# Hybrid decoder trunk on one core: the last down projection as seven block products with stored weight sums

## The chip, the cores and the metric

The kernel runs on one core of a Trainium2 chip (NeuronCore). A core has a matrix engine (TensorE, PE in the profile), whose weight loads are listed apart as PEld, a vector engine (VectorE, DVE), a scalar engine (ScalarE, ACT), a general engine (GpSimd, POOL) and a queue engine (SyncE, SP). Each engine executes its instructions in the order in which they stand in its queue; a wait of one instruction holds everything behind it. Transfers to and from DRAM are issued by SP, ACT or POOL and run on 16 DMA engines. The metric is the device time of the whole kernel in microseconds (us).

## What is computed

Two decoder layers (`DEPTH = 2`) on 512 rows of 1024 channels, each with a token mixer of three branches and a gated feed-forward, then one RMS norm. The change touches the feed-forward of both layers and the last norm:

```python
def conv_ffn(h, w_up, conv_w, conv_b, w_down):      # D_FF = 2816
    u = h @ w_up                                      # (512, 1024) @ (1024, 5632)
    c = conv_b + causal depthwise convolution of width 3 over the rows of u
    gate, val = jnp.split(c, 2, axis=-1)
    return (jax.nn.silu(gate) * val) @ w_down         # (512, 2816) @ (2816, 1024)

for l in range(DEPTH):
    ...                                               # token mixer, x = x + ... @ w_out
    x = x + conv_ffn(rmsnorm(x, norm2_g[l]), ffn_w_up[l], ...)
return rmsnorm(x, final_g)
```

## The kernel before

Every product in single precision is made of three matmuls on split operands: an operand is a pair of tiles, `hi` (rounded to the matmul format) and `lo` (the remainder), and `mm3` issues lo times hi, hi times hi and hi times lo, each with a 128x128 stationary operand and 512 moving columns.

Weights come through a plan. `unit` hands out the next weight block of 128x512. `load` fetches it with a DMA on SP into one of three raw buffers (`NRAW = 3`, tile `wr`), and `part` splits it: ScalarE casts the raw tile to `hi` (L135), VectorE subtracts (L136) and so frees the raw tile. The results go to pairs of tiles, `wh`/`wl` (three pairs) or `sh`/`sl` (from the pools `f`, `r` or `u`). `AHEAD` says how many units may be split ahead of the one in use. The position of an instruction in its engine's queue is chosen by a scheduler at build time, except where `keep_in_program_order` pins it (in the last stage TensorE is pinned).

The feed-forward has two stages. `ffn_up` makes 44 column blocks (22 pairs of gate and value, channels on partitions, the 512 rows along the free axis); each takes two weight units and 24 matmuls. VectorE multiplies by the norm factor (`fu`, L1054, straight from the accumulator in PSUM), ScalarE starts the convolution (L1056), VectorE adds its two other taps (L1057, L1058) and makes the gated product (`fth`, L1063 and L1064); the product is split into `ah` (L1066, L1067). In the second layer eight blocks of the residual are also turned to row order on the way (`xt`, through DRAM on POOL's queue, L226 and L230). `ffn_down` (first layer) takes 22 of these products for each of 8 column blocks, with weights `wdn`.

The second layer's down projection is `last`. It works with rows on partitions: `act` is the stationary operand, 128 of the 512 rows at a time (four row blocks), and the moving operand is a unit of 512 columns of `wdt`. For the first 512 columns all 22 steps of the inner dimension run over four accumulators in the pool `acc`, then the same for the other 512 columns in four accumulators of the pool `sm`. The last six units (`KEPT = 6`) are held, so that the row blocks end one after the other: each adds the residual (`add`, L1106, four pieces of 128 columns), squares and sums (L1109), gets its factor by a square root (L1137) and a reciprocal (L1138), is scaled and written out. Only the last row block's tail is left when the matmuls are over.

```python
pss = [self.acc() for _ in range(NC)]
for k in range(NFF):
    w = self.unit("wdt", 0, k, 0)
    for c in range(NC):
        prod(pss[c], k, c, w)
```

Of the kernel before, what the change touches and what calls it, by code (L numbers as in the profile page):

```python
# [8 lines left out]
F32 = mybir.dt.float32  # L9
# [15 lines left out]
KEPT = 6  # L25
SEQ = "0 H 0 S 0 U S U S 0 S 0 0 S 2 2 Y 0 0 2 1 2 1 2 1 2 1 2 1 2 1 1 1"
NRAW = 3
AHEAD = {None: 2, "p": 4, "r": 3, "f": 3, "u": 5}
# [20 lines left out]
class Emit:  # L49
# [68 lines left out]
    def load(self, u):  # L118
        name, l, i, c0, n, _ = u
        raw = self.wp.tile([128, 512], F32, name=self.nm("wr"), tag="wr", bufs=NRAW)  # L120
        with self.tc.high_priority():
            self.kept(self.nc.sync.dma_start(raw[:, :n], self.a[name][l, i][:, c0:c0 + n]))
        self.raws.append(raw)
        self.nraw += 1

    def part(self, u):
        raw, n, pool = self.raws.pop(0), u[4], u[5]

        self.turn = (self.turn + 1) % 5 if pool == "p" else 4
        if pool is None or self.turn < 3:  # L130
            hi, lo = [self.wp.tile([128, 512], F32R, name=self.nm(t), tag=t, bufs=3) for t in ("wh", "wl")]
        else:
            hi, lo = [{"f": self.f, "r": self.r, "u": self.u, "p": self.u}[pool](dt=F32R, n=t) for t in ("sh", "sl")]
        with self.tc.high_priority() if pool in (None, "p") else nullcontext():
            self.kept(self.nc.scalar.copy(hi[:, :n], raw[:, :n]))  # L135
            self.kept(self.nc.vector.tensor_tensor(lo[:, :n], raw[:, :n], hi[:, :n], op=SUB))  # L136
# [11 lines left out]
    def mm3(self, ps, w, x, start, stop):  # L148
        (wh, wl), (xh, xl) = w, x

        def mm(*x, **y):
            i = self.nc.tensor.matmul(*x, **y)  # L152
# [79 lines left out]

    def norm_new(self):
# [67 lines left out]
    def run(self):  # L301
        nc, tc, a, V = self.nc, self.tc, self.a, self.nc.vector
        self.con = self.cp.tile([128, NCC], F32, name="con")
        self.rst = self.cp.tile([128, 512], F32, name="rst")
# [729 lines left out]
    def ffn_up(self, l, st, x):  # L1034
# [4 lines left out]
        def at():  # L1039
# [4 lines left out]
        first = self.firstF(l, (78, 79, 80), st, (3,))  # L1044
        for i in range(NFF):
            if x and i % 2 == 1 and i < 17:
# [18 lines left out]
            hi, lo = at(), at()  # L1065
            A.copy(hi, th)  # L1066
            V.tensor_tensor(lo, th, hi, op=SUB)  # L1067
            act.append((hi, lo))
        return act

    def ffn_down(self, l, act, x, st):
# [3 lines left out]
        for m in range(8):  # L1075
# [7 lines left out]
            xd.append(d)  # L1083
        return x, xd


    def last(self, act):


        nc, V, A, P, po = self.nc, self.nc.vector, self.nc.scalar, self.nc.gpsimd, self.tc.keep_in_program_order  # L1090
        fg = [self.u(n="fg") for _ in range(2)]
        for h in range(2):
            nc.sync.dma_start(fg[h], self.a["fgr"][:, 512 * h:512 * h + 512].to_broadcast([128, 512]))
# [3 lines left out]
        def prod(ps, k, c, w):  # L1097
            cs = slice(128 * c, 128 * c + 128)
            ah, al = act[k]
            self.mm3(ps, (ah[:, cs], al[:, cs]), w, k == 0, k == NFF - 1)  # L1100

        def add(y, ps, j, c):

            b = slice(j % 4 * 128, j % 4 * 128 + 128)
            q = lambda t: t[:, b].rearrange("p (a d) -> p a d", d=32)
            return V.scalar_tensor_tensor(q(y), q(ps), 0.5, self.xt[j][:, c], op0=MUL, op1=ADD)  # L1106
# [3 lines left out]

        self.pool = None
        pss = [self.acc() for _ in range(NC)]
        for k in range(NFF):
            w = self.unit("wdt", 0, k, 0)
            for c in range(NC):
                prod(pss[c], k, c, w)
        ya = []
        for c in range(NC):
            y = self.u(n="ya")
            for j in range(4):  # L1120
                add(y, pss[c], j, c)
            square(y, ss[:, c:c + 1])
            P.tensor_tensor(y, y, fg[0], op=MUL)
            ya.append(y)
        V.tensor_scalar(bias, ss, 1.0 / D, 1e-6, op0=MUL, op1=ADD)
        pss = [self.sm() for _ in range(NC)]
        for k in range(NFF - KEPT):
            w = self.unit("wdt", 0, k, 512)
            for c in range(NC):
                prod(pss[c], k, c, w)  # L1130
        self.pool = "u"
        ws = [self.unit("wdt", 0, k, 512) for k in range(NFF - KEPT, NFF)]

# [7 lines left out]
        for c in range(NC - 1):  # L1141
            for k, w in enumerate(ws, NFF - KEPT):
                prod(pss[c], k, c, w)
            y, s = self.u(n="yb"), self.small((128, 1), "fs1")
            for j in range(4, 8):
                po(add(y, pss[c], j, c))
            po(square(y, s))
            rs = factor(s, bias[:, c:c + 1])
            po(A.activation(ya[c], ya[c], AF.Copy, scale=rs))
            nc.scalar.dma_start(self.a["out"][c, :, 0:512], ya[c])  # L1150
            po(V.scalar_tensor_tensor(y, y, rs, fg[1], op0=MUL, op1=MUL))
            nc.sync.dma_start(self.a["out"][c, :, 512:1024], y)
        c, y, b = NC - 1, self.u(n="yb"), bias[:, NC - 1:]
        for k, w in enumerate(ws, NFF - KEPT):
            prod(pss[c], k, c, w)
        for j in range(4, 8):
            po(add(y, pss[c], j, c))
        s = [self.small((128, 1), f"fs{i}", 1) for i in (2, 3)]
        for i in range(2):
            po(square(y[:, 256 * i:256 * i + 256], s[i]))  # L1160
        po(V.scalar_tensor_tensor(b, s[0], 1.0 / D, b, op0=MUL, op1=ADD))
        rs = factor(s[1], b)
        for i in range(2):
            h = slice(256 * i, 256 * i + 256)
            po(V.scalar_tensor_tensor(y[:, h], y[:, h], rs, fg[1][:, h], op0=MUL, op1=MUL))
            nc.sync.dma_start(self.a["out"][c, :, 512 + 256 * i:768 + 256 * i], y[:, h])
            po(A.activation(ya[c][:, h], ya[c][:, h], AF.Copy, scale=rs))
            nc.scalar.dma_start(self.a["out"][c, :, 256 * i:256 * i + 256], ya[c][:, h])
# [114 lines left out]
```

## Time and profile before

| what | value |
|---|---|
| three runs | 1714.98, 1713.65, 1714.87 us; median 1714.87 |
| profiled execution, first to last instruction | 1712.1 us |
| granted TensorE clock, mean | 1.000 |
| matmuls | 10280 |
| DMA, whole execution | 219.61 MB, mean 128 GB/s |
| second layer's `ffn_up`, about | 1359 to 1585.7 us |
| `last`, matmuls | 1585.7 to 1705.5 us |

The runs are timed without the profiler; the span of the profile is one other execution, from its first to its last instruction. The span lies 2.8 us under the median of the runs, which also hold what lies around it. A row of a group of instructions gives busy time, the mean of one in ns, the idle time of the engine just before them, and what ended it. A row of the timeline gives start, duration, engine, line and operation, and in brackets the idle time before it with its releaser. Two instructions of one engine may overlap in these rows, since the engines are pipelined: the distance of the starts says what one more instruction costs.

### The profile page before, as it was taken

What the parts mean: (1) busy time and instruction counts of PE and PEld (TensorE: products, weight loads), DVE (VectorE), ACT (ScalarE), POOL (GpSimd) and SP (SyncE); (2) the same over time, 40 slices, a digit from 0 to 9 for tenths busy, and PEclk for the clock granted to TensorE, in tenths of its full rate; (3) what the DMA queues carried; (4) which work ended last, traced back from release to release, by engine and by line L of the source; (5) the groups of instructions that cost most, each with busy time, mean ns of one, the idle gap of its engine ahead of it and who ended that gap; (6) DMA issues with size and microseconds to landing.
All of it is one profiled execution on the core that took longest, in us unless ns stands there. A gap on an engine that the chain in (4) does not pass through costs nothing.

```text
span 1712.1 us, 27377 instructions
## 1 busy us (share of the span) xinstructions
PE 1701.0 (99%) x10280; PEld 1392.4 (81%) x10280; DVE 1155.0 (67%) x1998; ACT 774.9 (45%) x1315; POOL 178.2 (10%) x213
## 2 busy tenths in 40 slices
PE   9999999999999999999999999999999999999998
PEld 7888777788888888888888888777888888888886
DVE  6887745578669777753368887555776787787333
ACT  6563443554255444433355634345533554444223
POOL 2121000003200000000021210100141011100010
PEclk9999999999999999999999999999999999999999
DMA  5236553525542333233432365535254433333333
GB/s 180 87 109 205 174 174 99 178 89 163 163 148 93 98 99 96 69 113 114 123 105 87 107 222 168 159 122 178 77 185 147 137 122 117 113 109 99 99 99 105
DMA packets 132325, 219.61 MB, mean 128 GB/s; under 512 B 16864, under 2 KB 37088, under 8 KB 132192
## 3 DMA queue, kind: packets, MB, share of 16 engines
q1 hardware_dynamic: 116336, 180.94, 34.4%
q0 software_dynamic: 6784, 20.98, 3.8%
q10 hardware_dynamic: 9072, 15.94, 2.6%
q8 instruction: 81, 1.33, 0.3%
q14 instruction: 52, 0.43, 0.1%
HBM read 188.43 MB, written 29.36 MB: 127 GB/s over the span
## 4 chain that ended last, share of the span: by engine, by line
PE 89%; DMA 5%; DVE 3%; ACT 1%; issue 1%; SPq 1%; ACTq 0%; POOL 0%; DVEq 0%; POOLq 0%
PE acc L152 80%; PE sm L152 4%; PE sm L640 2%; DMA wr<-wall 2%; PE sm L893 1%; DVE wl L136 1%; PE sm L547 1%; DMA ws<-sgw 1%; DMA tr<-yt 0%; DMA tr<-bkT 0%; SPq L226 0%; DMA bkS<-tr 0%; PE sm L998 0%; DMA x<-xT 0%; DMA tr<-qkt 0%
## 5 line engine op out<-in xcount | busy, mean ns | idle before, releaser
L152 PE MATMUL acc<-hi,sh 128*128 128x512 f32 x1108 | 431.9, 390 | 0.0
L152 PE MATMUL acc<-lo,sh 128*128 128x512 f32 x1108 | 431.6, 390 | 0.0
L152 PE MATMUL acc<-hi,sl 128*128 128x512 f32 x1108 | 430.6, 390 | 0.0
L135 ACT CAST sh<-wr 128x512 fp32r<-128x512 f32 (+1 forms) x347 | 212.2, 615 | 356.6 <-PE acc L152 264.3
L136 DVE TENSOR_TENSOR sl<-wr,sh 128x512 fp32r<-128x512 f32 (+1 forms) x347 | 236.1, 683 | 139.9 <-ACT sh L135 74.9
L136 DVE TENSOR_TENSOR wl<-wr,wh 128x512 fp32r<-128x512 f32 x233 | 165.2, 710 | 184.9 <-ACT wh L135 182.3
L135 ACT CAST wh<-wr 128x512 fp32r<-128x512 f32 x233 | 144.1, 619 | 281.1 <-PE acc L152 182.3
L152 PEld LDWEIGHTS acc<-hi,sl 128*128 128x128 f32 x1108 | 208.0, 188 | 43.7 <-DVE gth L1013 0.3
L152 PEld LDWEIGHTS acc<-lo,sh 128*128 128x128 f32 x1108 | 208.0, 188 | 43.6 <-issue 0.9
L152 PEld LDWEIGHTS acc<-hi,sh 128*128 128x128 f32 x1108 | 208.0, 188 | 43.6 <-issue 0.3
L152 PE MATMUL acc<-lo,wh 128*128 128x512 f32 x588 | 232.5, 395 | 0.5 <-DVE lo L211 0.3
L152 PE MATMUL acc<-hi,wl 128*128 128x512 f32 x588 | 230.3, 392 | 0.5 <-DVE wl L136 0.5
L152 PE MATMUL acc<-hi,wh 128*128 128x512 f32 x588 | 229.5, 390 | 0.0
L152 PEld LDWEIGHTS acc<-lo,wh 128*128 128x128 f32 x588 | 110.5, 188 | 26.3 <-DVE lo L211 1.6
L152 PEld LDWEIGHTS acc<-hi,wl 128*128 128x128 f32 x588 | 110.5, 188 | 25.9 <-DVE wl L136 2.3
L152 PEld LDWEIGHTS acc<-hi,wh 128*128 128x128 f32 x588 | 110.6, 188 | 22.4 <-issue 0.2
L152 PE MATMUL acc<-ah,sh 128*128 128x512 f32 x352 | 108.4, 389 | 0.0
L1054 DVE TENSOR_TENSOR fu<-acc,rsF 128x512 f32<-128x512 f32 x88 | 60.6, 688 | 56.4 <-PE acc L152 56.3
L1056 ACT ACTIVATE cv<-fu,pc 128x512 f32<-128x512 f32 x88 | 71.6, 816 | 46.7 <-DVE fu L1054 44.4
L1057 DVE SCALAR_TENSOR_TENSOR cv<-fu,pc,cv 128x511 f32<-128x511 f32 x88 | 65.8, 748 | 21.1 <-ACT cv L1056 20.6
L152 PE MATMUL acc<-wl,hi 128*128 128x512 f32 x192 | 78.3, 408 | 0.0
L152 PEld LDWEIGHTS acc<-ah,sh 128*128 128x128 f32 x352 | 66.1, 188 | 13.7
(312 smaller groups left out, 2345.4 us busy)
## 6 DMA issues: line engine op xcount, KB each, us to landing
wr<-wall SPq DMA_DIRECT2D x488, 256.0 KB, 2.7
gd<-gth ACTq DMA_DIRECT2D x48, 256.0 KB, 3.0
gth<-gd POOLq DMA_DIRECT2D x48, 256.0 KB, 3.6
wr<-wdt SPq DMA_DIRECT2D x44, 256.0 KB, 2.6
wr<-wdn SPq DMA_DIRECT2D x40, 256.0 KB, 2.7
tr<-bkT SPq DMA_DIRECT2D x16, 256.0 KB, 2.8
bkS<-tr SPq DMA_DIRECT2D x128, 32.0 KB, 2.5
tr<-vT SPq DMA_DIRECT2D x8, 256.0 KB, 2.6
```

The lines of the kernel that those rows point to most:

```text
L135: self.kept(self.nc.scalar.copy(hi[:, :n], raw[:, :n]))
L136: self.kept(self.nc.vector.tensor_tensor(lo[:, :n], raw[:, :n], hi[:, :n], op=SUB))
L152: i = self.nc.tensor.matmul(*x, **y)
L547: i = T.matmul(pK[hv[1 - h], j, :], bk[hv[h], c, 1, :], x[hv[h], c, :], start=True, stop=True)
L640: po(T.matmul(o, l, r, start=start, stop=True, skip_group_check=True))
L893: po(T.matmul(X[h][:, i, :], lhsT, rhs, start=new[h], stop=stop, skip_group_check=True))
L1054: V.tensor_tensor(u, ps, self.rsF, op=MUL)
L1056: A.activation(t, u, AF.Identity, scale=self.p("cw2", j), bias=self.p("cb", j))
L1057: V.scalar_tensor_tensor(t[:, 1:], u[:, :511], self.p("cw1", j), t[:, 1:], op0=MUL, op1=ADD)
```

## The change

The down projection of the second layer, `Y = A W` with A of 512x2816 and W of 2816x1024, is cut into 2x2 blocks (rows in halves of 256, columns in halves of 512, the inner dimension in pairs of 128-channel steps), and the eight block products of each pair become seven, with sums of blocks on both sides (the Winograd form of Strassen's scheme). There are 11 pairs `q`, and seven products `p` of each; one product of one pair is a weight unit times two row blocks, that is six matmuls.

- Weight sums. For four of the seven products (`p` = 7, 5, 6, 4) the weight is a combination of the four blocks of the pair. `presum` makes these in the first layer's feed-forward: four loads of 128x512 on POOL's queue, four VectorE operations, four stores to DRAM (`tsum`) on POOL's queue, for one pair at a time (pairs 0 to 3 within `ffn_up`, on 16 tiles of pool `f`; pairs 4 to 10 within `ffn_down`, on tiles of pool `u`).
- Sums of the activations. `halves`, in the second layer's `ffn_up`, makes from two products the row-half combinations: four VectorE operations of 256 columns for a pair, two split operands instead of two, and three stores to DRAM on POOL's queue for what is needed later (`ab`: first row half of both; `s4`).
- `last`. A first pass runs p = 7, 5, 6, 4 over all pairs with eight accumulators (four of `acc`, four of `sm`). Meanwhile `spill` brings the stored `ab` back on POOL's queue and splits it. A second pass adds p = 1 to the accumulators of p = 6, a third runs p = 2, a fourth p = 3, each over 11 pairs. The combinations of the accumulators are made on ScalarE (`half`) and VectorE (`addx`, `plus`, plain additions) during these passes. Two row blocks are finished and written out during the p = 2 and p = 3 passes, with POOL's queue, the other two at the end as before, one after the other.
- Raw buffers. Units of the last stage (plan pool `q`) are fetched up to six ahead (`DEEP = 6`), every other one into a tile of pool `u`, and split four ahead, three pairs of five into `wh`/`wl` and two of five into tiles of pool `u`. The last six units still use the three raw buffers.
- The final gain's load (`fg`) moves from SP's to POOL's queue. `halves` takes its two work tiles from the same three `wh` and three `wl` tiles as the weights.

```diff
+PRE = {(0, "f", 2): 0, ..., (0, "d", 6): 10}
-AHEAD = {None: 2, "p": 4, "r": 3, "f": 3, "u": 5}
+AHEAD = {None: 2, "p": 4, "r": 3, "f": 3, "u": 5, "q": 4}
+DEEP = 6
...
-            while self.nraw < min(self.npart + NRAW, len(self.plan)):
+            while self.nraw < len(self.plan) and self.nraw < self.npart + (DEEP if self.plan[self.nraw][5] == "q" else NRAW):
...
-        raw = self.wp.tile([128, 512], F32, name=self.nm("wr"), tag="wr", bufs=NRAW)
+        raw = self.u(n="wr") if u[5] == "q" and self.nraw % 2 else self.wp.tile([128, 512], F32, name=self.nm("wr"), tag="wr", bufs=NRAW)
+        src = self.tsum[i] if name == "tsum" else self.a[name][l, i]
...
+    def presum(self, l, stage, m):
+        if self.pre:
+            q, b = self.pre.pop()
+            V = self.nc.vector
+            V.tensor_tensor(b[3], b[3], b[1], op=SUB)
+            V.tensor_tensor(b[1], b[1], b[0], op=SUB)
+            V.tensor_tensor(b[0], b[0], b[3], op=ADD)
+            V.tensor_tensor(b[2], b[2], b[0], op=SUB)
+            for p, t in zip((7, 5, 6, 4), (b[3], b[1], b[0], b[2])):
+                self.tsum[q, p] = self.dp.tile([128, 512], F32, name=self.nm("ts"))
+                self.nc.gpsimd.dma_start(self.tsum[q, p], t)
+        q = PRE.get((l, stage, m))
+        if q is not None:
+            b = self.fpre.pop(0) if stage == "f" else [self.u(n="pre") for _ in range(4)]
+            for i, t in enumerate(b):
+                self.nc.gpsimd.dma_start(t, self.a["wdt"][0, 2 * q + i // 2][:, i % 2 * 512:i % 2 * 512 + 512])
+            self.pre.append((q, b))
...
+    def halves(self, a, b, q, at):
+        V, P, h = self.nc.vector, self.nc.gpsimd, [slice(0, 256), slice(256, 512)]
+        s, d = [self.wp.tile([128, 512], F32, name=self.nm(t), tag=t, bufs=3) for t in ("wh", "wl")]
+        ab = self.dp.tile([128, 512], F32, name=self.nm("ab"))
+        ...
+        P.dma_start(ab[:, h[0]], a[:, h[0]])
+        P.dma_start(ab[:, h[1]], b[:, h[0]])
+        V.tensor_tensor(s[:, h[0]], a[:, h[1]], b[:, h[1]], op=ADD)
+        V.tensor_tensor(s[:, h[1]], s[:, h[0]], a[:, h[0]], op=SUB)
+        V.tensor_tensor(d[:, h[0]], b[:, h[0]], s[:, h[1]], op=SUB)
+        P.dma_start(self.s4[:, h[q % 2]], d[:, h[0]])
+        V.tensor_tensor(b[:, h[0]], a[:, h[0]], a[:, h[1]], op=SUB)
+        return self.split(s, at), self.split(b, at), ab, self.s4
...
+        def spill(src, n):
+            o = self.u(n="sp")
+            nc.gpsimd.dma_start(o[:, :n], src[:, :n])
+            hi, lo = self.f(dt=F32R, n="hi"), self.f(dt=F32R, n="lo")
+            A.copy(hi[:, :n], o[:, :n])
+            V.tensor_tensor(lo[:, :n], o[:, :n], hi[:, :n], op=SUB)
+            return hi, lo
...
+        for q in range(Q):
+            s, t = act[q][:2]
+            for p in (7, 5, 6, 4) if q < Q - 1 else (6, 7, 5, 4):
+                w = unit(p, q)
+                x, at = {7: (t, 0), 5: (s, 0), 6: (s, 256), 4: (t, 256)}[p]
+                for r in range(2):
+                    prod(pss[p][r], x, at, r, w, q == 0, q == Q - 1)
+            ...
+            if q:
+                ab.append(spill(act[q - 1][2], 512))
...
+        for q in range(Q):
+            ...
+            w = unit(1, q)
+            for r in range(2):
+                go(1, q, r, w)
+            ...
+            if q < 2:
+                v[2, q], v[3, q] = addx(pss[5][q], 1, 2 + q), addx(pss[5][q], 1, q)
+            elif q < 4:
+                v[1, q - 2] = addx(pss[4][q - 2], 0, q)
...
+        self.pool = "u"
+        ws = [unit(3, q) for q in range(Q - KEPT, Q)]
+        for r in range(2):
+            for q, w in enumerate(ws, Q - KEPT):
+                go(3, q, r, w)
+            ...
+            po(plus(y, out[3][r], y))
```

More of the change, by code (lines that the diff above doesn't have):

```diff
@@ L1102, in add, with unit, prod @@
[L1102 to L1106, printed above, removed]
+        def unit(p, q):
+            if p > 3:
+                return self.unit("tsum", 0, (q, p), 0)
+            return self.unit("wdt", 0, 2 * q + (p > 1), 512 * (p == 3))
+        def prod(ps, x, at, r, w, first, end, **kw):
+            cs = slice(at + 128 * r, at + 128 * r + 128)
+            self.mm3(ps, (x[0][:, cs], x[1][:, cs]), w, first, end, **kw)
@@ L1108, in square, with plus @@
+        def plus(y, ps, z):
+            return V.scalar_tensor_tensor(y, ps, 0.5, z, op0=MUL, op1=ADD)
         def square(y, s):
             return A.activation(self.u(n="sq")[:, 0:y.shape[1]], y, AF.Square, accum_out=s)
[L1111 to L1124, printed above, removed]
@@ L1139, in factor @@
             return rs
[L1141 to L1168, printed above, removed]
+        pss = {p: [(self.acc if p in (7, 5) else self.sm)() for _ in range(2)] for p in (7, 5, 6, 4)}
@@ new lines, in last @@
+        for q in range(Q - KEPT):
+            w = unit(3, q)
+            for r in range(2):
+                go(3, q, r, w)
+            if q in (1, 3):
+                r, y = q // 2, v[0, q // 2]
+                plus(y, out[2][r], y)
+                square(y, ss[:, r:r + 1])
+                V.tensor_scalar(bias[:, r:r + 1], ss[:, r:r + 1], 1.0 / D, 1e-6, op0=MUL, op1=ADD)
+                V.tensor_tensor(y, y, fg[0], op=MUL)
+        self.pool = "u"
+        ws = [unit(3, q) for q in range(Q - KEPT, Q)]
```

128 lines of the change are left out of this document (103 added, 25 removed).

## Prediction, on record before the changed kernel ran

> **What bounds the kernel now.** I read the page first, then the busy time by stretches, the groups by line, and the timeline of VectorE where `ffn_up` passes into `last`.
>
> ```profile
> span 1712.1 us, 27377 instructions
> PE 1701.0 (99%) x10280; PEld 1392.4 (81%) x10280; DVE 1155.0 (67%) x1998; ACT 774.9 (45%) x1315; POOL 178.2 (10%) x213
> PE 89%; DMA 5%; DVE 3%; ACT 1%; issue 1%; SPq 1%; ACTq 0%; POOL 0%; DVEq 0%; POOLq 0%
> 1359.16 286.64 PE acc L152 x1264
> 1585.70:1705.50 119.80, 119.80 (x530) 98.97 (x528) 43.14 (x82) 36.49 (x65) 5.95 (x4) 1.00 0.30 97
> ```
>
> The fourth line is a piece of the chain that ended last: matmuls without a break from the second `ffn_up` into `last`, 286.64/1264 = 0.2268 us each. The fifth is `last` alone: 528 matmuls in 119.8 us, 0.227 each, at full clock. VectorE is busy 43.1 us of them and ScalarE 36.5, DMA 30%. So the stage costs what its matmuls cost, and the two other engines have more than half of it free.
>
> **The matmuls removed.** Before: 22 steps x 8 blocks x 3 = 528. After: 7 products x 11 pairs x 2 row blocks x 3 = 462, of the same shape. 66 x 0.2268 = **15.0 us less**. The built order of the changed kernel has this count and the same matmuls elsewhere. A weight unit now feeds six matmuls, 1.36 us, where it fed twelve, 2.72.
>
> What can eat the gain is VectorE's queue, since it gets work in three places. Its price per instruction is the distance of starts when it isn't waiting:
>
> ```profile
> 1376.17 0.68 DVE L1067 TENSOR_TENSOR ah<-fth,ah 128x512 fp32r<-128x512 f32 x1
> 1376.77 0.68 DVE L136 TENSOR_TENSOR sl<-wr,sh 128x512 fp32r<-128x512 f32 x1
> 1377.38 0.74 DVE L1058 SCALAR_TENSOR_TENSOR cv<-fu,pc,cv 128x510 f32<-128x510 f32 x1
> 1378.04 0.68 DVE L1063 SCALAR_TENSOR_TENSOR fth<-fth,cv 128x512 f32<-128x512 f32 x1
> 1705.68 0.89 DVE L1106 SCALAR_TENSOR_TENSOR yb<-sm,xt 128x128 f32<-128x128 f32 x4 [1.13 <-PE sm L152]
> L1078 DVE SCALAR_TENSOR_TENSOR xi<-acc,xi 128x512 f32<-128x512 f32 x8 | 5.5, 685 | 7.7 <-PE acc L152 7.7
> ```
>
> 0.60 us for 512 columns, 0.66 for an operation with three operands (I take it for `plus` too, whose nearest row is L1078), 0.22 for 128 columns (0.89/4). 256 columns lie between 0.22 and 0.60; I take 0.36.
>
> **Weight sums in the first layer.** 44 VectorE operations x 0.60 = 26.4 us, and 88 DMAs of 256 KB on POOL's queue.
>
> ```profile
> 560.00:604.00 44.00, 44.00 (x196) 36.44 (x195) 34.13 (x54) 21.01 (x34) 0.00 (x0) 1.00 0.32 99
> 740.00:866.00 126.00, 126.00 (x558) 104.33 (x557) 50.97 (x85) 41.73 (x71) 4.32 (x8) 1.00 0.40 118
> ```
>
> In `ffn_up` four operations (2.4 us) come every two steps, 21.8 us, in which VectorE now idles (44 - 34.13)/44 = 22%, 4.9 us. In `ffn_down` it idles 75 of 126 us and gets 28 operations, 17 us. The loads stand a step ahead of the operations and nothing else waits in POOL's queue there. **0.** Without that cover it would be the 26.4 us; the lower end is 0, as nothing is removed.
>
> **End of the second `ffn_up`.** `halves` adds four operations of 256 columns for a pair, 1.4 us in 21.8; the average fits. But order decides at the end. After the last-but-three accumulator (released 1569.7) the built order has on VectorE: `fu` 0.60, half 0.36, `ah` 0.60, half 0.36, two taps 1.32, `ah` 0.60, and only then the weight part, 0.69 to its end: 1574.2. TensorE, 56 matmuls ahead of its 1585.7, wants it at 1573.0. **+1.3 us**, between 0 (if the part's place doesn't bind) and 2. The same adding up on the kernel before puts the parts of that place at 1570.33, without a wait of TensorE; the trace has
>
> ```profile
> 1570.32 1.28 DVE L136 TENSOR_TENSOR sl<-wr,sh 128x512 fp32r<-128x512 f32 x2
> ```
>
> **Passage into `last`.** After the last accumulator of `ffn_up` the rows before are:
>
> ```profile
> 1586.00 0.69 DVE L1054 TENSOR_TENSOR fu<-acc,rsF 128x512 f32<-128x512 f32 x1 [1.22 <-PE acc L152]
> 1587.58 0.75 DVE L1057 SCALAR_TENSOR_TENSOR cv<-fu,pc,cv 128x511 f32<-128x511 f32 x1 [0.89 <-ACT cv L1056]
> 1588.24 0.68 DVE L1063 SCALAR_TENSOR_TENSOR fth<-fth,cv 128x512 f32<-128x512 f32 x1
> ```
>
> Count from TensorE's first matmul of `last`. `fu` starts at 0.4 and the first tap at 2.0, after ScalarE. In the built order then come: tap, product, tap 1.98; the fifth unit's part 0.60; product 0.60; parts of units 9 and 10 1.2; two halves, each waiting for the one before, 0.8; the part of unit 14 0.60; a half 0.36; and then the part of unit 6, which ends at 2.0 + 6.1 + 0.7 = 8.8, with the hand-over 8.9. TensorE has five units before it, 6.8 us. **+2.1 us**, between 0 and 3.5 (durations instead of distances).
>
> **First pass.** Four units and a spill are 5 x 0.60 = 3.0 us of VectorE in 5.44 of TensorE, and about as much ScalarE:
>
> ```profile
> L135 ACT CAST sh<-wr 128x512 fp32r<-128x512 f32 (+1 forms) x347 | 212.2, 615 | 356.6 <-PE acc L152 264.3
> wr<-wdt SPq DMA_DIRECT2D x38, 256.0 KB, 2.6
> ```
>
> A raw tile comes back after six units, 8.2 us; load, cast and subtraction take 2.6 + 0.62 + 0.69 = 3.9. 256 KB in 1.36 us and a spill in 5.44 are 240 GB/s, 2.5 times the 97 GB/s that took 30% of the DMA engines: 74%. **0**, cover 4.3 us a unit; the loads may get slower, which is a rival's part.
>
> **Second and third pass.** Here VectorE gets the accumulators' work. Count from the end of the last pair's p = 6. In the built order up to the part for unit 53: 8 + 16 quarter operations 5.3, 8 weight parts 4.8, 5 spills 3.0 = 13.1, begun at 0.9 (ScalarE's copy of the sum first), with about 1.9 more of waits for ScalarE's copies and casts and 0.6 for the last end: 16.5. TensorE wants that unit at 11 x 1.36 = 15.0. +1.5. Then p = 1 ends, at 14 x 1.36 + 1.5 = 20.5; six `plus` wait for it, 4.0, and eight operations of 0.60 follow to the end of unit 62's part: 29.7 with the hand-over, where TensorE wants it at 20 x 1.36 + 1.5 = 28.7. Another +0.9. **+2.4 us**, between 0.4 (no waits for ScalarE) and 6.4 (durations 0.69, 0.75, 0.28).
>
> **The last six units.** They have three raw tiles, and in the built order the tile of unit 74 is that of unit 71, and the tile of 77 that of 74. Unit 71's part ends 41.1 us after the same point: 29.7 and ten parts 6.0, two `plus` 1.3, four scalings of finished row blocks 2.6, small ones and waits for ScalarE 1.5. Two rounds of load, cast and subtraction, with hand-overs 4.2 each, end at 49.5; TensorE takes three matmuls of each of these units at first, 0.68 us, and would want unit 77 at 30 x 1.36 + 5 x 0.68 = 44.2, with the 2.4 above 46.6. **+2.9 us**, between 0 (part 71 two us earlier) and 6.8 (both loads at the 4.8 us below). The kernel before held six units too, but with 2.72 us for a unit ahead of them.
>
> **Tail.** One 512-column addition instead of four pieces, and the first square sum waits for all of it: 0.69 instead of the 0.52 to 1706.20.
>
> ```profile
> 1706.20 0.42 ACT L1109 ACTIVATE sq<-yb 128x256 f32<-128x256 f32 x1 [1.61 <-DVE yb L1106]
> ```
>
> **+0.2 us.** The outputs on POOL's queue leave over 20 us before the end.
>
> **Sum:** -15.0 + 0 + 1.3 + 2.1 + 0 + 2.4 + 2.9 + 0.2 = -6.1 us. The profiled span goes from 1712.1 to 1706.0. The median of the runs, 2.8 us over the span, goes from 1714.87 to **1708.8**.
>
> **Rivals.**
>
> *All waits hidden.* The scheduler placed the parts so late because it counted on them; if the engines overlap better than my distances, only the tail remains: 1714.87 - 15.0 + 0.2 = 1700.1. For it: in the kernel before VectorE catches up everywhere, and TensorE never waits in this stretch. Against it: three of the four delays follow from the order alone.
>
> *VectorE at full durations and slower loads.* The upper ends of the middle terms together: -15.0 + 2 + 3.5 + 6.4 + 6.8 + 0.2 = +3.9 if all hit at once; two thirds of the way there from the forecast, 1715.5, no measurable change. For it: hand-overs between engines cost 0.1 to 0.3 us that I counted in few places; the DMA rate is one that the stage before never had. Against it: the check at 1570.32.
>
> *The spills hold the queues: slower.* 17 spills come on POOL's queue, and their cast and subtraction stand in the queues of ScalarE and VectorE ahead of weight parts that TensorE needs.
>
> ```profile
> L226 POOL DMA_DIRECT2D xt<-tr x32: 548/548/580, 1355.2 to 1513.3; - x32
> DMA to landing us min/median/max: 2.2/2.9/4.8
> 1402.00:1446.00 44.00, 44.00 (x196) 36.44 (x195) 34.45 (x54) 20.39 (x32) 5.46 (x10) 1.00 0.36 113
> ```
>
> Ten lie in the first pass, where VectorE has 2.4 us free per pair; seven in the passes after, where it has none. If each landed at 4.8 instead of 2.9, 7 x 1.9 = 13.3 us: 1722.1. It decides from 9.5 us on, 1.36 late each, a landing over 4.3 us. For it: the longest landing of such a transfer, and the issue order that puts spills shortly before their use. Against it: the median, and that POOL issues each in 0.55 us while VectorE is busy 78% of the stretch. The Trainium skill (SBUF — State Buffer, "Who interferes with whom") says that GpSimd and VectorE share a port pair which one of them holds for a whole instruction, and that a transfer issued by GpSimd can starve while VectorE holds it; its example goes from about 620 to 3100 ns. By that, an estimate, seven times 2.5 us would give 1726.3. The issue times of 548 to 580 ns above don't show it.
>
> That the change doesn't do what it says is closed by the count of matmuls.
>
> **How the numbers follow.** What a measurement of this kernel can tell from no change is 0.2%, 3.4 us: faster is below 1711.4, slower above 1718.3. My sum with its own range (1703 to 1711.4): 0.62. All hidden: 0.12. Full durations: 0.12, in the middle band. Spills: 0.14. Faster 0.74, same 0.12, slower 0.14. The forecast's own range leaves out 0.38; the first two rivals' bounds added, from 1701 to 1716, leave out about 0.2: half of the all-hidden case below, the spill case above.
>
> **What would show it.** In the profile after: the matmuls of `last` 66 fewer at 0.227 us (else the first term is wrong); no idle of TensorE between 511 and 866 (weight sums); idle of TensorE on a VectorE part once just before `last`, once at its sixth unit, some four times in the p = 1 and p = 2 passes, and one on a load shortly before the end; POOL landings near 2.9. The prediction is wrong if TensorE's waits in `last` sum to more than 12 us or less than 3, or if they name DMA on POOL's queue.

## The result

| kernel | median | lowest to highest | runs | ratio to before, 95% interval |
|---|---|---|---|---|
| before | 1714.67 us | 1712.9 to 1722.14 | 20 | |
| after | 1711.49 us | 1706.19 to 1715.82 | 20 | 0.9977, 0.9968 to 0.9986 |

By the ratio the change takes off 3.9 us (2.4 to 5.5 by the interval), by the medians 3.2; the prediction asked for 3.4 to call it a difference, so the change is clear of zero and on the edge of that. Forecast were 6.1. The runs of the changed kernel spread over 9.6 us, where 18 of the 20 runs of before lie within about 4. The profiled execution took 1706.19 us, the shortest of the twenty, so its trace alone doesn't explain the median. A second profiled execution (below) took 1713.66.

Each run has the mean granted clock of TensorE on record: 0.999 in 6 of the 20 runs of the changed kernel, as in both profiled executions, 0.998 in 10 and 0.997 in 4. In the traces of the experiments each 0.001 below 0.999 goes with one stretch of some 3.4 us at a clock of 0.50 ahead of the last matmul (experiment 5 shows what that is). So most runs probably held such a stretch, which neither trace of this kernel shows.

From the page after, the span, the engines, the shares of the chain that ended last, and POOL's DMA queue (packets, MB, share of the 16 engines' time; 20.98 MB and 3.8% before):

```profile
span 1704.5 us, 27880 instructions
PE 1687.8 (99%) x10214; PEld 1379.2 (81%) x10214; DVE 1233.0 (72%) x2157; ACT 798.0 (47%) x1367; POOL 249.8 (15%) x353
DMA 2%; DVE 2%; ACT 1%; PE 1%; issue 1%; ACTq 0%; DVEq 0%; SPq 0%
q0 software_dynamic: 17216, 54.28, 9.5%
```

There are 66 matmuls fewer, as counted. The chain is followed back only to the first pass of `last` here (its shares sum to 7% of the span), and in this stretch it goes through loads and VectorE as much as through TensorE, where before it was matmuls without a break. The chain of waits in order of time shows how (start, duration, what). Near the start of `last`, in the middle, and at its end:

```profile
1596.88 4.30 DMA wr<-ts
...
1601.20 0.63 ACT sh L139
...
1601.86 0.70 DVE sl L140
...
1602.58 3.96 DMA wr<-ts
...
1610.54 4.92 DMA wr<-ts
...
1682.01 3.72 DMA wr<-wdt
...
1688.41 2.60 DMA wr<-wdt
...
1691.68 0.70 DVE sl L140
1692.43 5.11 PE acc L156 x21
```

Load, cast, subtraction, and at once the next load into the raw tile that the subtraction freed: one round takes 4.30 + 0.63 + 0.70 and hand-overs, 5.7 us. The next takes 8.0 us (1602.58 to 1610.54), since subtractions of other parts stand between in VectorE's queue; six units last 8.2. This is the ring of raw tiles, the wait that the prediction had for the last six units only; loads through it are on the chain in the first pass too.

The landing times say why. After, in `last` (count, size, and the median us from issue to landing):

```profile
wr<-ts SPq DMA_DIRECT2D x35, 256.0 KB, 4.0
wr<-wdt SPq DMA_DIRECT2D x33, 256.0 KB, 3.4
sp<-ab POOLq DMA_DIRECT2D x11, 256.0 KB, 4.4
sp<-s POOLq DMA_DIRECT2D x5, 256.0 KB, 4.8
```

The forecast had 2.6 for a weight load, the median of the kernel before. The Trainium skill (SBUF — State Buffer, "The DMA setup-cost knee") fits a transfer as about 2 us plus its bytes over 436 GB/s, which gives an estimate of 2.6 us for 256 KB. The trace of before agrees with that at 30% of the DMA engines' time. In this trace, at the shares shown next, the medians are 4.0 for the stored sums (most of them loaded at 80%) and 3.4 for `wdt`, so the measured time decides there and the fit is too short.

The busy time of the engines in three stretches of `last` (first 50 us, next 25, rest), the first execution: stretch, its length, then busy us and count for PE, PEld, DVE, ACT, POOL, the clock, the DMA share and GB/s.

```profile
1587.52:1637.52 50.00, 47.64 (x209) 38.80 (x208) 33.86 (x57) 27.45 (x50) 7.50 (x14) 1.00 0.80 271
1637.52:1662.52 25.00, 24.70 (x108) 19.82 (x107) 19.37 (x55) 14.43 (x27) 2.15 (x4) 1.00 0.64 220
1662.52:1697.52 35.00, 34.43 (x149) 27.36 (x147) 27.86 (x51) 19.31 (x41) 2.17 (x4) 1.00 0.45 147
```

The same stretches of the second execution of the same kernel:

```profile
1589.51:1639.51 50.00, 47.37 (x207) 38.43 (x206) 32.95 (x56) 26.98 (x50) 7.39 (x14) 1.00 0.79 264
1639.51:1664.51 25.00, 21.94 (x92) 16.54 (x91) 14.95 (x44) 12.70 (x25) 2.27 (x5) 1.00 0.65 212
1664.51:1705.00 40.49, 39.20 (x167) 30.39 (x165) 33.18 (x64) 21.16 (x44) 2.17 (x4) 1.00 0.42 140
```

`last` took 110.0 us in the one and 115.5 in the other, where 462 matmuls of 0.2268 are 104.8. The count of matmuls is the better measure here, since a matmul that starts late counts as busy for part of its wait. An undisturbed `last` (experiment 9) has 221 and 111 in the first two stretches. So the first execution is 12 and 3 matmuls behind, 2.7 and 0.7 us, and loses 1.8 in the rest (5.2 in all); the second 14 and 19, 3.2 and 4.3, and loses 3.2 in the rest. The greatest difference between the two, 3.6 us, is in the middle stretch, where the first pass passes into the second.

ScalarE's timeline at that place, the first execution (in brackets the idle time before, with its releaser):

```profile
1640.64 0.62 ACT L139 CAST sh<-wr 128x512 fp32r<-128x512 f32 x1 [3.41 <-DMA wr<-wdt]
1641.17 1.82 ACT L139 CAST wh<-wr 128x512 fp32r<-128x512 f32 x3
1645.77 1.14 ACT L139 CAST sh<-wr 128x512 fp32r<-128x512 f32 x2 [2.78 <-DMA wr<-wdt]
1646.82 0.59 ACT L1162 ACTIVATE v<-sm 128x512 f32<-128x512 f32 x1
```

and the second:

```profile
1646.07 0.62 ACT L139 CAST sh<-wr 128x512 fp32r<-128x512 f32 x1 [6.19 <-DMA wr<-wdt]
1646.59 1.66 ACT L139 CAST wh<-wr 128x512 fp32r<-128x512 f32 x3
1653.06 1.14 ACT L139 CAST sh<-wr 128x512 fp32r<-128x512 f32 x2 [4.81 <-DMA wr<-wdt]
1654.11 0.59 ACT L1162 ACTIVATE v<-sm 128x512 f32<-128x512 f32 x1
```

The order in the queue is the same, the loads are not. The load behind the first bracket, in the chain of the first execution and in that of the second:

```profile
1636.52 4.10 DMA wr<-wdt
```

```profile
1639.39 6.66 DMA wr<-wdt
```

and two of the waits that come of it, in TensorE's timeline of the second:

```profile
1654.75 0.50 PE L156 MATMUL sm<-sl,hi 128*128 128x512 f32 x1 [0.90 <-ACT v L1162]
1661.08 0.50 PE L156 MATMUL sm<-wl,hi 128*128 128x512 f32 x1 [0.93 <-DVE wl L140]
```

The casts stand ahead of `half` (L1162) in ScalarE's queue. `half` must read the sums of p = 6 before p = 1 may add to them, so TensorE waits for ScalarE, which waits for a load. `half` starts 64.6 us into the stage (1654.11 - 1589.51) and not 59.3 as in the first execution. VectorE's work on the accumulators begins that much later, and from there VectorE is busy without a gap for 15 us in both, so the delay isn't made up.

### The profile page after: what moved, and what is told of

The parts are those of the page before. It is cut to its first block, busy times and chain, and to the rows that moved or that the text cites. A ratio compares the mean times of both kernels' runs of the same rounds, so it can differ in the third digit from the quotient of the medians.

```text
span 1704.5 us, 27880 instructions
## 1 busy us (share of the span) xinstructions
PE 1687.8 (99%) x10214; PEld 1379.2 (81%) x10214; DVE 1233.0 (72%) x2157; ACT 798.0 (47%) x1367; POOL 249.8 (15%) x353
## 5 line engine op out<-in xcount | busy, mean ns | idle before, releaser
L139 ACT CAST sh<-wr 128x512 fp32r<-128x512 f32 (+1 forms) x375 | 228.0, 615 | 394.9 <-PE acc L156 225.2
L140 DVE TENSOR_TENSOR sl<-wr,sh 128x512 fp32r<-128x512 f32 (+1 forms) x375 | 254.8, 685 | 129.4 <-ACT sh L139 92.8
L156 PE MATMUL acc<-wl,hi 128*128 128x512 f32 x212 | 86.1, 406 | 0.0
L156 PE MATMUL acc<-wh,lo 128*128 128x512 f32 x212 | 82.8, 390 | 0.0
L156 PE MATMUL acc<-wh,hi 128*128 128x512 f32 x212 | 82.7, 390 | 0.0
```

The costliest lines, as they stand in the source:

```text
L156: i = self.nc.tensor.matmul(*x, **y, **kw)
```

## The experiments

Each was timed in interleaved runs with the kernel before on the same chip. Medians are set beside before's of the same chip: 1715.81 us for the first four, 1716.88 for 5 to 8, 1715.65 for 9 to 11, 1715.83 for 12.

**1. The changed kernel again** (no edit).

> The changed kernel once more, for a second profiled execution: the first one (1706.19 us) was the fastest of the twenty, 5.3 us under their median. Theory A: what differs from run to run lies in `last`, where transfers fill 0.81 of the DMA engines' time and a raw tile comes back just in time; median 1710 to 1713, and a profiled execution above 1709 shows more idle time of TensorE between 1590 and 1698 than the 3.3 us of the first, behind casts that wait for a load. Theory B: it lies in the first layer, where the loads for the weight sums (235 GB/s) hold up weight loads in some runs; then the idle time stands between 500 and 870. Theory C: nothing in particular, the runs of this kernel spread anyhow; then before's runs on this chip spread as widely (9 us from lowest to highest).

1713.4 us, 1710.37 to 1715.41, ratio 0.9981 (0.9972 to 0.9989). Theory A's place was right in the main: from 500 to 870 TensorE has no idle time in either execution, and the difference in `last` is the one shown above. Theory C isn't excluded: before's runs on this chip reach from 1713.7 to 1723.19 us, though 29 of the 31 lie within 4.5 us, and the 11 runs here within about 5. And the executions differ outside `last` too. The norm's reciprocal ahead of the second `ffn_up` starts (timeline of before, of after, and of this execution)

```profile
1359.92 3.39 DVE L265 RECIPROCAL rsF<-rms 128x128 f32<-128x128 f32 x4 [2.46 <-ACT rms L261]
```

```profile
1360.40 3.39 DVE L288 RECIPROCAL rsF<-rms 128x128 f32<-128x128 f32 x4 [2.47 <-ACT rms L284]
```

```profile
1362.38 3.39 DVE L288 RECIPROCAL rsF<-rms 128x128 f32<-128x128 f32 x4 [2.47 <-ACT rms L284]
```

and `last` begins 227.1 us later in both, 1.3 more than before. So 2.0 us of the difference of 7.5 arise earlier (in the experiments below this point lies between 1360.9 and 1366.3), 5.5 in `last`.

**2. No weight sums**, and **12. no weight sums, whole tiles.** In 2, the first layer's loads, VectorE operations and stores for the sums go, and `last` loads pieces of `wdt` instead. In 12, it loads tiles of 128x512 that lie contiguous in DRAM, as the sums do.

```diff
-        if self.pre:
+        if False:
...
         if q is not None:
+            for p in (7, 5, 6, 4):
+                self.tsum[q, p] = self.a["wdt"][0, 2 * q + (p > 5)][:, p % 2 * 512:p % 2 * 512 + 512]
+        if False:
...
-        if l == 0:
+        if False:
```

In 12 the first layer's work is left out in the same way, and the source of the load is:

```diff
-        src = self.tsum[i] if name == "tsum" else self.a[name][l, i]
+        src = self.gd[self.nraw % 3, self.nraw % 8] if name == "tsum" else self.a[name][l, i]
```

> The weight sums are left out: no loads, no VectorE operations, no stores for them in the first layer, and `last` loads plain blocks of the weights in their place, of the same size and number. So the products with sums are not the reference's. Theory A (`last` sets the spread and the sums are hidden): median within 1.0 us of the changed kernel on this chip, the same spread. Theory B (the sums' traffic in the first layer costs): 3 to 5 us less than the changed kernel, and runs within 4 us of each other.

> As in the kernel without sums, no weight sums are made; the 44 units of the first pass now load whole 256 KB tiles from DRAM (gate tiles that the second layer has stored), contiguous as the stored sums are, and not 2 KB pieces of 4 KB rows. The queues of `last` are the same in all three. So the products with sums are not the reference's. If the piecewise source made the kernel without sums slower: back to the changed kernel's 0.998 of before, `last` near 110 to 115 us. If it was something else (that the sums' work in the first layer is missing, or the chance of the runs): as without sums, 0.9996 and 116 to 118.

Without sums 1716.14 us, 0.9996 (0.9985 to 1.0007): 2.7 slower than with them in experiment 1, with intervals that overlap a little, which no theory had. With whole tiles 1711.87, 0.9975 (0.9963 to 0.9986), the changed kernel's 0.9977 to 0.9981 again. So the sums' work in the first layer costs nothing that can be measured, and where the first pass reads from does cost: 4.3 us by the medians, 3.6 by the ratios, whose intervals just touch. The landings in a stretch of the first pass, without sums and then with whole tiles:

```profile
wr<-wdt SPq DMA_DIRECT2D x31, 256.0 KB, 4.6
sp<-ab POOLq DMA_DIRECT2D x9, 256.0 KB, 6.4
```

```profile
wr<-gd SPq DMA_DIRECT2D x31, 256.0 KB, 3.8
sp<-ab POOLq DMA_DIRECT2D x11, 256.0 KB, 5.2
```

The order in the queues of VectorE and ScalarE in `last` is the same in these two kernels and the changed one. ScalarE's two waits for loads where the first pass passes into the second, 6.2 us together in the first execution, 8.8 with whole tiles, 11.0 in the second execution and 11.6 with pieces, go with stages of 110.0, 114.1, 115.5 and 117.9 us. That is four executions, in the order of their loads' landing. The landing isn't all: in the two without sums TensorE waited 2.3 and 2.7 us once (with whole tiles at the sixth unit, with pieces behind ScalarE's second wait), and its granted clock stood at 0.50 for some 3.4 us soon after, which by the starts of the matmuls is about 1.6 us of each stage. With that taken off, the order of the four stays, and so does the difference between these two.

**3. Six raw tiles for the last six units too.** Their plan pool gets a name of its own (`k`), which is fetched as `q` is.

```diff
-        raw = self.u(n="wr") if u[5] == "q" and self.nraw % 2 else ...
+        raw = self.u(n="wr") if u[5] in ("q", "k") and self.nraw % 2 else ...
...
-        self.pool = "u"
+        self.pool = "k"
```

> The last six units of `last` get raw tiles like the units before them (six deep, every second one from the u pool) in place of three; nothing else is changed. The prediction's term for these units was +2.9 us, from two rounds of load, cast and subtraction of 4.2 us each on three raw tiles. If it holds in full: 2.9 us less than the changed kernel. In the first profiled execution TensorE idles 0.65 us between 1680 and 1697.6, so by that execution only 0.6 us less; in slower executions, where the loads land later, up to 3.5. Rival: the six units wait for VectorE and not for tiles: no change (within 0.5).

1711.53 us, 0.9972 (0.9962 to 0.9982): 1.9 under experiment 1, with intervals that overlap. The profiled execution has 150 matmuls in its last 34.1 us, with TensorE busy throughout, so the waits there are gone; what the medians can tell of the size stays between 0 and 2.9.

**4. More traffic in the first pass.**

```diff
                 ab.append(spill(act[q - 1][2], 512))
+                for t in ab[-1]:
+                    nc.gpsimd.dma_start(self.dp.tile([128, 512], F32R, name=self.nm("ex")), t)
```

> In the first pass of `last`, after each spill's split, its two halves are also written to DRAM by POOL's queue (20 transfers of 256 KB, some 90 GB/s more over the pass); nothing reads them. The scheduler also moves some weight parts by a place or two. Theory A: DMA share above 0.95 in that pass, weight loads at 5 us or more, and the time 4 to 12 us above the changed kernel, with the idle time of TensorE in the first pass behind loads. If VectorE's order alone sets the stage: within 1.5 us.

1714.08 us, 0.9991 (0.9979 to 1.0003): 0.7 above experiment 1, not 4 to 12. The DMA share rose to 0.93 in the first 50 us and 0.91 in the next 25, loads of the sums to 4.9 us (from 3.9 in experiment 1), and still the median hardly moved. As a measure of the DMA engines' rate this speaks against theory A; since the scheduler also moved weight parts, it isn't clean.

**5. The halves' work tiles from the u pool.**

```diff
-        s, d = [self.wp.tile([128, 512], F32, name=self.nm(t), tag=t, bufs=3) for t in ("wh", "wl")]
+        s, d = self.u(n="hs"), self.u(n="hd")
```

> The work tiles s and d of `halves` come from the u pool, and no longer from the wh and wl tiles, of which there are three each and which the weight parts need too. With that the built order puts three weight parts ahead of the last pair's halves, where they stood behind. In both profiled executions of the changed kernel TensorE waits 1.8 us for the seventh unit's part, 6.3 us into `last`, and the second ffn_up takes 227.1 us from its norm's reciprocal to `last`, 1.2 more than before. Theory (the forecast's two terms of +1.3 and +2.1, with the shared tiles as their cause): both waits go, 2.5 to 3.2 us less than the changed kernel. Rival: VectorE's work itself is too much at that place, and the wait comes back a few units later: less than 1 us.

1712.5 us, 0.9976 (0.9966 to 0.9985): no gain. The wait at the sixth unit went, and in the profiled execution (1716.61 us, the longest of the nine) another came, in which TensorE stands for 6.8 us until 1605.62. VectorE's timeline there:

```profile
1601.35 0.69 DVE L149 TENSOR_TENSOR ah<-hs,ah 128x512 fp32r<-128x512 f32 x1 [0.22 <-ACT ah L148]
1604.54 0.43 DVE L1114 TENSOR_TENSOR fth<-fth 128x256 f32<-128x256 f32 x1 [2.49 <-DMA ab<-fth]
1604.88 1.29 DVE L140 TENSOR_TENSOR sl<-wr,sh 128x512 fp32r<-128x512 f32 x2
```

The last operation of `halves` overwrites the columns of `b` that are on their way to `ab`, so it waits for that store to be done, 2.49 us, and two weight parts wait behind it. In the changed kernel weight parts stand between, and the same overwrite (1598.71) has no wait for the store. TensorE's first matmul after its wait, and one of those that follow:

```profile
1605.62 0.80 PE L156 MATMUL acc<-sl,ah 128*128 128x512 f32 x1 [6.80 <-DVE sl L140]
1607.07 0.63 PE L156 MATMUL acc<-sl,ah 128*128 128x512 f32 x1
```

Elsewhere in `last` such a row lasts 0.39 us. The granted clock is 0.50 from 1602 to about 1608.8, and until then the matmuls start 0.43 us apart in place of 0.23: this wait cost more than its length. The traces of experiments 2, 3, 8, 10 and 12 have such a stretch too.

**6 and 11. Nine raw tiles** in `last`, the last six units included.

```diff
-DEEP = 6
+DEEP = 9
...
-        raw = self.u(n="wr") if u[5] == "q" and self.nraw % 2 else ...
+        raw = self.u(n="wr") if u[5] in ("q", "k") and self.nraw % 3 else ...
```

> Nine raw tiles in place of six in `last` (two of three from the u pool), and for the last six units too. Two profiled executions of the changed kernel, with the same order, took 110.0 and 115.5 us for `last`; in the second, one weight load issued near the end of the first pass took 6.66 us in place of 4.10, the casts behind it stood still, and with them the copies of p = 6's sums, which stand behind those casts in ScalarE's queue. Theory L (late single loads, which a raw tile that comes back after six units can't hide): with nine, the load has 12.2 us in place of 8.2, stage 107 to 111, median 3 to 5 us less than the changed kernel and a smaller spread. Theory V (VectorE's queue sets the stage, loads only follow): less than 1 us. Theory R (the DMA engines' rate sets it): the same or slower, with longer landings.

> The nine-tile kernel again, on the chip of the two above. As before: 0.993 to 0.994 of before, runs within 2 us of each other.

1705.62 us, 0.9935 (0.9923 to 0.9947), and again 1706.11, 0.9947 (0.9935 to 0.9958); runs within 1.9 us of each other both times. The three stretches of the first of the two:

```profile
1588.82:1638.82 50.00, 47.91 (x210) 39.06 (x209) 35.76 (x59) 29.10 (x52) 7.82 (x15) 1.00 0.83 284
1638.82:1663.82 25.00, 25.00 (x111) 20.58 (x111) 20.46 (x55) 14.14 (x27) 2.15 (x4) 1.00 0.69 226
1663.82:1696.44 32.62, 32.62 (x144) 26.58 (x142) 25.57 (x48) 18.00 (x39) 2.18 (x4) 1.00 0.31 104
```

and its landings:

```profile
wr<-ts SPq DMA_DIRECT2D x34, 256.0 KB, 4.7
wr<-wdt SPq DMA_DIRECT2D x33, 256.0 KB, 4.0
```

The loads land later than with six tiles (4.7 and 4.0 for 4.0 and 3.4), at a higher DMA share, and the middle and the last stretch have no wait left. The trace of experiment 11 has a little in the middle one, five matmuls or 1.1 us:

```profile
1638.62:1663.62 25.00, 24.45 (x106) 19.47 (x105) 20.16 (x56) 14.03 (x27) 2.37 (x5) 1.00 0.70 224
```

So neither the rate of the DMA engines nor VectorE's amount of work set the time there. What the edit gives is an earlier start of a load before its use; the scheduler also moved weight parts and spills by up to four places in the two queues, so the ring isn't all that differs. Theory A in its first form, the DMA share, falls; theory L fits, with a gain of 5 to 8 us by the ratios where it had 3 to 5. All ten runs have a mean granted clock of 0.999, so the stretches at 0.50 are gone as well.

**7. No spill loads.** The spills' casts read a tile that is in SBUF.

```diff
-            o = self.u(n="sp")
-            nc.gpsimd.dma_start(o[:, :n], src[:, :n])
+            o = act[0][0][0]
```

> The 17 spill loads of `last` are left out: their cast and subtraction read a tile that is in SBUF already, so the products p = 1, 2 and 3 are not the reference's; the stores in ffn_up stay. Theory L in the form that the spills' transfers make the weight loads late (8.3 instead of 12.2 transfers per 10 us): weight loads land at 3.0 us or less, the wait at the end of the first pass goes, stage 107 to 110, median 3 to 5 us less than the changed kernel. If the weight loads alone make themselves late: within 1.5 us, with a stage that still varies by 5 us.

1707.94 us, 0.9951 (0.9938 to 0.9963), some 5 under the changed kernel. Its weight loads land at

```profile
wr<-ts SPq DMA_DIRECT2D x34, 256.0 KB, 3.2
wr<-wdt SPq DMA_DIRECT2D x33, 256.0 KB, 3.1
```

and the middle stretch has 111 matmuls. Less traffic and a deeper ring mend the same stretch: with six tiles the spills' transfers make the weight loads land later. How much of the 5 us is theirs isn't separated, since the scheduler also put the spills' splits earlier, by up to fifteen weight units.

**8. Nine raw tiles and the halves' tiles together.**

> Both edits together: nine raw tiles, and the halves' work tiles from the u pool. If the two effects add: 6 to 8 us less than the changed kernel, stage about 106, 0.994 of before. If VectorE's queue is the next limit, less than their sum.

1710.28 us, 0.9963 (0.9951 to 0.9976): worse than nine tiles alone. TensorE waits 3.7 us once, at the place of experiment 5's wait, and goes on at a clock of 0.50.

**9 and 10. The last pair's halves later**, with nine and with twelve raw tiles. The `halves` of the last pair alone are called in `last`, at q = 1, with work tiles from the u pool.

```diff
-            else:
+            elif i < NFF - 1:
                 act.append(self.halves(even, th, i // 2, at))
+            else:
+                self.late = lambda: self.halves(even, th, i // 2, at)
+                act.append(None)
...
             if q == 1:
+                act[Q - 1] = self.late()
```

> Nine raw tiles, and the halves of the last pair alone are made a pair of units into `last` (its tiles from the u pool), so that they come off VectorE's queue ahead of the first weight parts of `last`. In the nine-tile kernel TensorE still waits 1.5, 1.0 and 0.6 us in the first 13 us of `last`, where VectorE is busy 0.9 of the time. Theory: VectorE's work at that place is the limit, and 2.7 us of it can go later; 1 to 3 us less than the nine-tile kernel. Rival: the three taps and products of ffn_up's last step, which can't be put off, set it: within 0.7 us.

> The same with twelve raw tiles (three of four from the u pool). If the load's lateness is covered by nine, no further gain: within 1 us of the nine-tile kernel with late halves; if some loads are still late, 1 to 2 us less.

1703.93 us, 0.9932 (0.9919 to 0.9945), and 1703.92, 0.9936 (0.9922 to 0.9951): 2.2 less than nine tiles on this chip, and nothing more from twelve. The stretches of nine:

```profile
1591.44:1641.44 50.00, 50.00 (x221) 41.15 (x220) 36.01 (x59) 29.58 (x53) 9.12 (x17) 1.00 0.84 287
1641.44:1666.44 25.00, 25.00 (x111) 20.45 (x110) 20.56 (x55) 14.34 (x27) 2.15 (x4) 1.00 0.70 238
1666.44:1696.81 30.37, 30.37 (x134) 24.70 (x132) 24.66 (x47) 17.39 (x38) 2.17 (x4) 1.00 0.26 87
```

TensorE never stops in `last` of experiment 9: 105.4 us. This kernel beats before and the changed one: 11.7 us under before, three times the gain of the change as it was made.

## Why the prediction was right, and where it was not

The median lies 0.1 us above the forecast's own range (1703 to 1711.4) and within the wider one (1701 to 1716); the forecast of 1708.8 lies 2.7 us below it. The way was right, and "faster" by the 3.4 us that the prediction asked for is not settled. Term by term, in the first and in the second execution:

| term | forecast | first | second |
|---|---|---|---|
| ahead of the second `ffn_up` | none | +0.5 | +2.5 |
| end of `ffn_up` | +1.3 | +1.3 | +1.3 |
| matmuls removed | -15.0 | -15.0 | -15.0 |
| waits in `last` (2.1 + 0 + 2.4 + 2.9) | +7.4 | +5.2 | +10.7 |
| tail | +0.2 | +0.4 | +0.4 |
| sum | -6.1 | -7.6 | -0.1 |

The spans are 1704.5 and 1712.0 against 1712.1, and the sums agree with them. That the forecast came near the median is in part luck: one execution gained more than forecast and the other nothing, and within `last` the first pass, put at 0, cost something in both, while the two terms behind it came out smaller than forecast in the first execution and larger in the second.

- **Matmuls and weight sums: right.** 66 fewer, 0.2262 us each where nothing stops (50.00/221). The sums cost 0, by experiment 12.
- **End of `ffn_up`: right**, 1.3 us in both executions. VectorE's part for the weights ended at 1574.64 in the first (1573.95 + 0.69), where the forecast, with the 0.5 us from ahead of it, had 1574.7.
- **Passage: right in place and near in size.** The sixth unit was to come 8.9 us after the first matmul, 2.1 late. It came at 8.75, after 1.79 us of waiting:

```profile
1596.27 0.50 PE L156 MATMUL acc<-wl,ah 128*128 128x512 f32 x1 [1.79 <-DVE wl L140]
```

  Experiment 5 moved this wait. Nine tiles still have 1.49 us there (experiment 6), and experiment 9 removed it, with the last pair's halves out of VectorE's queue at that place.
- **First pass: the step that failed.** "0, cover 4.3 us a unit" took 2.6 us for a load, from a stage at 30% of the DMA engines' time. At 80% the median is 4.0 in the stored sums, and the load at the pass's end took 6.66 in the second execution. The round of 3.9 us became one of 5.7 and more, and casts and subtractions queue behind the one that is late. Of the 2.7 and 3.2 us lost in the first 50 us, the 1.79 and 1.76 at the passage leave 0.9 and 1.4 for this pass; the greater cost of its late loads, 4.3 us in the second execution, falls into the stretch behind it. The forecast left slower loads to a rival, "full durations and slower loads" (1715.5): of its two halves the loads were real, and the median lies between it and the forecast. The 0.1 to 0.3 us that it gave for a hand-over between engines didn't show: in the round of 5.70 us above, 0.07 is left for all of them.
- **Second and third pass: right that VectorE is full, wrong in what decides.** TensorE lost 0.7 us in the first execution's middle stretch and 4.3 in the second's, where VectorE's work on the accumulators began 5.3 us later. With nine tiles TensorE waits nowhere in the middle stretch of experiment 6, and 1.1 us in that of experiment 11, so VectorE's work itself didn't need the 2.4 us.
- **Last six units: the mechanism right**, as the chain shows. The stretch that holds them lost 1.8 us in the first execution and 3.2 in the second, and nothing with six tiles (experiment 3), whose median is 1.9 lower, with intervals that overlap; the forecast's 2.9 is possible and not shown.
- **The spills rival: its price partly true, by another way.** The spills landed above its 4.3 us, at 4.4 and 4.8, without the 13 us. In neither trace of the changed kernel does a cast of a spill wait for its load, so they didn't hold the queues of ScalarE and VectorE in that way. Without their loads the kernel took some 5 us less (experiment 7), with weight loads that landed earlier and another order. POOL issued them without delay (duration in ns, least, median and greatest):

```profile
L1154 POOL DMA_DIRECT2D sp<-ab x11: 536/536/541, 1586.4 to 1631.4; - x11
```

  The Trainium skill's rule (SBUF — State Buffer, "Who interferes with whom"), by which VectorE can starve a transfer that GpSimd issues, would have given 1726.3 us by the estimate in the prediction. These issue times don't show it, at a VectorE busy for 33.86 of 50 us. The same section of the Trainium skill says that the delay was seen beside a `tensor_copy` and not beside a `tensor_tensor`. VectorE's weight parts and spill splits here are `TENSOR_TENSOR` rows; the estimate left that out.

Not settled: why the time up to the second `ffn_up` varies by 2 us and more from one execution to the next, and what each of the other runs held. A part is seen: in the traces of experiments 3, 5 and 10 TensorE waits 2.2 to 2.4 us near 1110 us, and 3.4 us at a clock of 0.50 follow. Where the runs of the changed kernel with a mean clock below 0.999 had such a stretch isn't known.

## What to carry to other kernels

A load's landing time is that of the stage in which it will run: where a change multiplies the traffic, give the ring of raw tiles room for the slowest load there, not for the median of the stage before it; here three more tiles (and the same depth for the last six units) were worth more than the change had brought by itself. When work is moved ahead of waiting instructions in an engine's queue, look at what else those instructions wait for: here a copy out of PSUM behind a cast that waited for a load, and an overwrite that waited for a store. Price a long wait of TensorE above its length: here the clock fell with some of them. A trace of the fastest of many runs shows the kernel at its best; where runs spread, take a second one before the causes are named, and compare the clock of the traced runs with that of the others.

## What the runs showed of the hardware

- Two executions of one kernel, with the same queues, had a 256 KB load of 4.10 us and of 6.66 us at the same place; the DMA share was 0.64 and 0.65 in the 25 us in which they landed.
- Loads of 128 pieces of 2 KB, each half of a 4 KB row, landed at 4.6 us, where contiguous tiles of the same size landed at 3.8 in the same stretch; the kernel took 1716.14 in place of 1711.87 us.
- Landings got longer with more loads outstanding (4.0 to 4.7 and 3.4 to 4.0 us), and the time shorter.
- After TensorE had waited 2.2 to 6.8 us, its granted clock stood at 0.50 in the traces of experiments 2, 3, 8, 10 and 12, for some 3.4 us, and in that of experiment 5, for some 6.8 us, half of them within the wait; matmuls of 512 columns then started 0.43 us apart in place of 0.23. It did not after 2.29 us in experiment 7, nor after 1.8 us in the changed kernel.
- An operation of VectorE that overwrites what a store is still reading waited 2.49 us for that store (experiment 5).
